# Splitting the first 4 MB load of a streaming GELU kernel by rows: 16 rows, then 112

## The chip, the cores and the metric

The kernel runs on one core of one Trainium2 chip. The metric is the device time of one execution in microseconds, as the median over several executions. Every load and store is issued by the sync engine and carried row by row by 16 DMA engines: the records of the kernel before hold 1408 packets of one row each, and 176 of 4 bytes, 16 for each of the 11 transfers. Landing times are those that the profile records.

## The reference

```python
def reference(x, y):                      # both float32, 1024 x 4096
    z = x + y
    return (0.5 * z * (1 + np.tanh(np.sqrt(2 / np.pi) * (z + 0.044715 * z ** 3)))).astype(np.float32)
```

33.55 MB are read and 16.78 MB written, with a dozen operations per element: a streaming kernel.

## The kernel before

The tensors are seen as 128 partitions of 32768 numbers. x and y come in four slabs of 128 x 8192 each (4.19 MB, 32 KB a row), alternately, all on the sync engine's queue. GpSimd adds (VectorE adds the first chunk), ScalarE and VectorE compute the GELU in chunks of 2048 columns, and three stores write the result. `begin_early` moves the first loads ahead of the program's opening barrier.

```python
    xv, yv, ov = (a.rearrange("(p n) d -> p (n d)", p=P) for a in (x, y, out))
    loads = [8192, 8192, 8192, 8192]
    stores = [16384, 10240, 6144]
    # ... (cut)
    zt = pool_sb.tile([P, TOT], fp32, tag="z", name="z")

    def load_x(i):
        a, b = lr[i]
        nc.sync.dma_start(out=zt[:, a:b], in_=xv[:, a:b])

    def load_y(i):
        a, b = lr[i]
        s, o = divmod(a, YS)
        if o == 0:
            yt[s] = pool_y.tile([P, YS], fp32, tag="y", name=f"y{s}")
        nc.sync.dma_start(out=yt[s][:, o : o + b - a], in_=yv[:, a:b])
    # ... (cut: stores, add, square, multiply-add, sigmoid, multiply; the order of issue)
    sp = []
    for i in range(len(loads)):
        sp += [(load_x, i), (load_y, i)]
    sp += [(store, i) for i in range(len(stores))]
    # ... (cut)
    tc.compile()
    begin_early(nc, 2)
    wait_late(nc)
```

Of the kernel before, what the change touches and what calls it, by code (L numbers as in the profile page):

```python
# [10 lines left out]
def begin_early(nc, count):  # L11


    head, body = (b.instructions for b in nc.main_func.blocks[:2])
    SP = mybir.EngineType.SP
    moved = [i for i in body if i.engine == SP and isinstance(i, mybir.InstDMACopy)][:count]
    assert not any(i.sync_info and i.sync_info.on_wait for i in moved)
    assert all(i.regs_accessed() == ((), ()) for i in moved)
    at = next(k for k, i in enumerate(head) if i.engine == SP)
    for k, i in enumerate(moved):  # L20
        body.remove(i)
        head.insert(at + k, i)


def wait_late(nc):



    body, end = (b.instructions for b in nc.main_func.blocks[1:3])
    last = [i for i in body if isinstance(i, mybir.InstDMACopy)][-1]  # L30
    (sem,) = [u.id for u in last.sync_info.on_update]
    all_done = end[0]
    reset = next(i for i in end if isinstance(i, mybir.InstDrain) and i.is_reset_sema)
    at = end.index(reset)
    clear = end[at + 1]
    first, stop = reset.reset_range_start, reset.reset_range_stop
    assert all_done.engine == mybir.EngineType.SP and reset.engine == mybir.EngineType.Pool
    assert isinstance(clear, mybir.InstISA) and clear.engine == mybir.EngineType.Pool
    waits = all_done.sync_info.on_wait
    (its,) = [w for w in waits if w.id == sem]  # L40

    end[0] = mybir.InstDrain(
        name=all_done.name, engine=all_done.engine, debug=all_done.debug, is_reset_sema=False,
        sync_info=mybir.SyncInfo(on_wait=[w for w in waits if w.id != sem], on_update=[]),
    )
    parts = []
    for f, e in ((first, sem), (sem + 1, stop)):
        if f < e:
            nc.gpsimd.sem_clear(range(f, e))
            parts.append(nc.cur_bb.bb.instructions.pop())  # L50
    end[at + 1 : at + 2] = parts
    end.append(
        mybir.InstEventSemaphore(
            name=clear.name, engine=mybir.EngineType.Activation, debug=clear.debug,
            sync_info=mybir.SyncInfo(
                on_wait=[its],
                on_update=[
                    mybir.SyncUpdate(
                        sync_type="semaphore", id=sem, ant_name=its.ant_name,
                        update_mode="sem-sub-imm", update_value=its.wait_value,  # L60
                    )
                ],
            ),
        )
    )
# [3 lines left out]
def kernel(  # L69
# [14 lines left out]
    nc = tc.nc  # L84
    P = nc.NUM_PARTITIONS
# [7 lines left out]
    xv, yv, ov = (a.rearrange("(p n) d -> p (n d)", p=P) for a in (x, y, out))  # L93
# [29 lines left out]
    zt = pool_sb.tile([P, TOT], fp32, tag="z", name="z")  # L123
    yt, wt, muls = {}, {}, {}

    def load_x(i):
        a, b = lr[i]
        nc.sync.dma_start(out=zt[:, a:b], in_=xv[:, a:b])  # L128

    def load_y(i):  # L130
        a, b = lr[i]
# [52 lines left out]
    for i in range(len(loads)):  # L184
        sp += [(load_x, i), (load_y, i)]
# [4 lines left out]
    for c in range(0, C, 2):  # L190
        dve += [(stt, c), (stt, c + 1), (mul, c), (mul, c + 1)]
        acts += [(sig, c), (sig, c + 1)]
        if c + 2 < C:
# [7 lines left out]
            if lr[i][0] % YS == 0  # L201
        ],
        add: lambda c: [(f, i) for i in over(lr, *cr[c]) for f in (load_x, load_y)],
        sq: lambda c: [(add, c)] + ([(mul, c - PS)] if c >= PS else []),
        stt: lambda c: [(sq, c)],
# [22 lines left out]
    ctx.close()  # L228
    tc.close()
    tc.compile()  # L230
    begin_early(nc, 2)
    wait_late(nc)


# [28 lines left out]
```

## Time and profile before

| | |
|---|---|
| time, beside the changed kernel | 120.62 us median (120.43 to 120.77, 4 runs) |
| span in the profile | 118.7 us |
| busiest compute engine | VectorE, 62% of the span |
| DMA engines occupied | 98.8% of 16 times the span |
| first load of x landed | 12.0 us |
| first load of y landed, and the first add began | 21.75 us, 21.85 us |

The table is read from below: the first add cannot start before the first slabs of x and y are there, and from the first row to the last, loads and stores occupy the 16 DMA engines almost without a gap (98.8%). The lines are shown and read in the prediction.

### The profile page before, as it was taken

To read this page: it belongs to the slowest core of one execution; us is meant where nothing else is said; L and a number is where in the kernel's file an instruction comes from. 1 tells how busy PE (TensorE), PEld (TensorE's weight loads), DVE (VectorE), ACT (ScalarE), POOL (GpSimd) and SP (SyncE) were. 2 spreads that over 40 slices of the span, in tenths; PEclk is the share of its full clock that TensorE was granted. 3 is DMA by queue.
4 is the path that set the end of the run, shared out by engine and by line. 5 is a ranking of instruction groups with operands and counts; after the bars stand their busy time and mean duration, and the time that the engine had idled before them with its cause. 6 is when DMAs were issued, how large, how long until landed. Compare 5 with 4: busy or idle time off the path is not lost.

```text
span 118.7 us, 172 instructions
## 1 busy us (share of the span) xinstructions
DVE 73.7 (62%) x35; ACT 61.0 (51%) x34; POOL 69.6 (59%) x19
## 2 busy tenths in 40 slices
DVE  0000000635799995739999968999994999990000
ACT  5000000063888965197698647888839779810000
POOL 0000000699996099999959999959999990000000
DMA  8989898989999898989999898998899889999896
GB/s 254 453 364 519 353 530 353 497 386 453 431 409 475 364 519 353 530 353 475 409 409 475 364 519 353 530 530 353 353 508 552 353 353 442 442 442 442 381 414 265
DMA packets 1584, 50.33 MB, mean 424 GB/s; under 512 B 176, under 2 KB 176, under 8 KB 176
## 3 DMA queue, kind: packets, MB, share of 16 engines
q1 hardware_dynamic: 1584, 50.33, 98.8%
HBM read 33.55 MB, written 16.78 MB: 424 GB/s over the span
## 4 chain that ended last, share of the span: by engine, by line
DMA 51%; POOL 26%; POOLq 4%; DVE 4%; DVEq 2%; ACT 2%; issue 0%; SPq 0%
DMA y<-in_y_dram 51%; POOL z L152 26%; POOLq L230 4%; DVE w L163 2%; DVEq L230 2%; DVE z L175 2%; ACT w L157 2%; SPq L128 0%; POOLq L152 0%
## 5 line engine op out<-in xcount | busy, mean ns | idle before, releaser
L152 POOL TENSOR_TENSOR z<-z,y 128x2048 f32<-128x2048 f32 x15 | 69.4, 4659 | 28.2 <-DMA y<-in_y_dram 28.2
L157 ACT ACTIVATE w<-z 128x2048 f32<-128x2048 f32 x16 | 30.1, 1882 | 37.6 <-DVE z L152 21.4
L163 DVE SCALAR_TENSOR_TENSOR w<-w,z 128x2048 f32<-128x2048 f32 x16 | 36.7, 2296 | 11.2 <-ACT w L157 11.0
L175 DVE TENSOR_TENSOR z<-w,z 128x2048 f32<-128x2048 f32 (+1 forms) x17 | 35.9, 2155 | 0.0
L168 ACT ACTIVATE w<-w 128x2048 f32<-128x2048 f32 x16 | 29.7, 1855 | 4.4 <-DVE w L163 4.3
L152 DVE TENSOR_TENSOR z<-z,y 128x2048 f32<-128x2048 f32 x1 | 2.3, 2293 | 20.5 <-DMA y<-in_y_dram 20.5
L215 ACT ACT_TABLE_LOAD x1 | 1.3, 1283 | 1.3 <-PEq L247 1.3
L214 DVE MEMSET one<- 128x1 f32 x1 | 0.1, 59 | 1.3 <-PEq L247 1.3
L247 POOL MEMSET const-float32-0.0<- 128x1 f32 x1 | 0.1, 99 | 0.2 <-issue 0.2
L215 ACT ACTIVATE one<-one 128x1 f32<-128x1 f32 x1 | 0.2, 203 | 0.0
L247 POOL MEMSET const-bfloat16-1.0<- 128x1 bf16 x1 | 0.1, 102 | 0.0
L247 POOL MEMSET const-uint8-127<- 128x1 uint8 x1 | 0.1, 102 | 0.0
L247 POOL MEMSET const-float32-1.0<- 128x1 f32 x1 | 0.1, 99 | 0.0
## 6 DMA issues: line engine op xcount, KB each, us to landing
z<-in_x_dram SPq DMA_DIRECT2D x4, 4096.0 KB, 31.3
y<-in_y_dram SPq DMA_DIRECT2D x4, 4096.0 KB, 22.2
out_dram<-z SPq DMA_DIRECT2D x1, 5120.0 KB, 15.8
out_dram<-z SPq DMA_DIRECT2D x1, 3072.0 KB, 11.9
out_dram<-z SPq DMA_DIRECT2D x1, 22.0
```

The costliest lines, as they stand in the source:

```text
L152: eng.tensor_add(out=zt[:, a:b], in0=zt[:, a:b], in1=yt[s][:, o : o + b - a])
L157: nc.scalar.activation(out=wt[c], in_=zt[:, a:b], func=act.Square, scale=root)
L163: nc.vector.scalar_tensor_tensor(out=wt[c], in0=wt[c], scalar=c1, in1=zt[:, a:b], op0=alu.add, op1=alu.mult)
L168: nc.scalar.activation(out=wt[c], in_=wt[c], func=act.Sigmoid)
L175: ins = nc.vector.tensor_mul(out=zt[:, a + o : a + o + n], in0=wt[c][:, o : o + n], in1=zt[:, a + o : a + o + n],)
L214: nc.vector.memset(one, 0.0)
L215: nc.scalar.activation(out=one, in_=one, func=act.Sigmoid)
L230: tc.compile()
L247: nc = _bacc.Bacc("TRN2", target_bir_lowering=False, num_devices=1)
```

## The change

The intent: a small transfer at the head of the queue, one row for each of the 16 DMA engines, might let the engines begin sooner than one of 128 rows. All bytes, and all work on the compute engines, stay.

```diff
     def load_x(i):
         a, b = lr[i]
-        nc.sync.dma_start(out=zt[:, a:b], in_=xv[:, a:b])
+        for r in (slice(0, 16), slice(16, P)) if i == 0 else (slice(0, P),):
+            nc.sync.dma_start(out=zt[r, a:b], in_=xv[r, a:b])
...
-    begin_early(nc, 2)
+    begin_early(nc, 3)
```

## The prediction

> **What bounds the kernel now.** I read the page first: the engine line, the slices, the DMA queue, the chain, the issues.

> ```profile
> span 118.7 us, 172 instructions
> DVE 73.7 (62%) x35; ACT 61.0 (51%) x34; POOL 69.6 (59%) x19
> ...
> DMA  8989898989999898989999898998899889999896
> ...
> q1 hardware_dynamic: 1584, 50.33, 98.8%
> ...
> DMA 51%; POOL 26%; POOLq 4%; DVE 4%; DVEq 2%; ACT 2%; issue 0%; SPq 0%
> ...
> out_dram<-z SPq DMA_DIRECT2D x1, 5120.0 KB, 15.8
> out_dram<-z SPq DMA_DIRECT2D x1, 3072.0 KB, 11.9
> out_dram<-z SPq DMA_DIRECT2D x1, 22.0
> ```

> No compute engine is above 62%, while packets occupy the 16 DMA engines for 98.8% of 16 times the span. 1.2% of 118.7 us is 1.4 us per DMA engine without a packet, start and end together. So the transfers are the bound, and nothing that leaves bytes and packet rate alone can win more than 1.4 us. The chain gives POOL 26%, which misleads: it steps through the adds because the waits allow it, not because the queue ran dry. The proof is in the times from issue to landing, from the view of tile y:

> ```profile
> L135 SPq DMA_DIRECT2D y<-in_y_dram x4: 328/376/464, 0.4 to 59.3; - x4
> ...
> DMA to landing us min/median/max: 20.7/22.2/39.5
> ```

> 50.33 MB in 0.988 x 118.7 = 117.3 us is 429 GB/s, 26.8 GB/s for each of 16 engines; a 4.19 MB load then takes 9.8 us, and one 32 KB row on one engine 1.22 us. The quickest y load needed 20.7 us from issue to landing, so it always had some 11 us of older work ahead. The three stores (8.39, 5.24 and 3.15 MB: 19.6, 12.2 and 7.3 us at that rate) landed after 22.0, 15.8 and 11.9 us: each was issued with 2.4 us or more still queued. The queue is never empty in the middle. A change of the first load therefore moves everything behind it by the same amount: what the first load loses or gains is the result.

> Then the start, as a table of stretches (duration; busy of DVE, ACT, POOL; clock; DMA share; GB/s, a packet being counted where it begins):

> ```profile
> 0.00:1.00 1.00, 0.00 (x0) 0.00 (x0) 0.20 (x4) 1.00 0.00 0
> 1.00:2.00 1.00, 0.06 (x1) 0.74 (x1) 0.00 (x0) 1.00 1.85 524
> 2.00:3.00 1.00, 0.00 (x0) 0.74 (x2) 0.00 (x0) 1.00 0.61 262
> 3.00:4.00 1.00, 0.00 (x0) 0.00 (x0) 0.00 (x0) 1.00 0.62 262
> 4.00:5.00 1.00, 0.00 (x0) 0.00 (x0) 0.00 (x0) 1.00 1.21 524
> ```

> and the timeline of the first two issues:

> ```profile
> 0.00 0.38 SPq L128 DMA_DIRECT2D z<-in_x_dram  x1
> ...
> 0.43 0.42 SPq L135 DMA_DIRECT2D y<-in_y_dram  x1
> ```

> The issue takes 0.38 us and no packet begins before 1.00. 524 GB/s in one microsecond is 0.524 MB, 16 rows of 32 KB: one first row per engine, all begun between 1.0 and 2.0. Their share of 1.85 says a first row took 1.85 us on average, 0.6 more than the steady 1.22[...]. In the packet records behind this table the first rows begin between 1.01 and 1.51 us, so the last engine starts 0.5 us after the first. This spread is what the change aims at.

> [...]

> **The change part by part.** Same bytes, same instructions on DVE, ACT and POOL; a comparison of the instruction orders shows one more transfer on the sync queue, ahead of everything, and nothing else moved.

> 1. Added: one issue, 0.38 to 0.45 us of the sync engine at the start. The y load is issued at about 0.9 instead of 0.43 us; it is not needed by the engines before about 11. Hidden.
> 2. Added: one completion write per engine. Loads land 9.7 us apart, 8 rows of 1.21 plus hardly anything; I estimate 0.03 us.
> 3. Gain:[...] The last engine sets the end, so at most 0.5 us; I estimate 0.25.
> 4. Cost, if the ports bind:[...]

> Sum: with ports binding 120.5 + 4.8 to 8.4 - 0.25 = 125.1 to 128.7, with 123.9 at the lowest (3.6 alone); without, 120.5 + 0.03 - 0.25 = 120.3.

> **The rivals.**
> - Hidden or a small gain (120.3). For it: the per-engine rate I see (26.8) is as well explained by the DMA engine as by the port[...].
> - Port contention (124 to 129).[...] Against: only that nothing here has shown it.
> - A gap between the small and the large transfer:[...] The second issue follows the first by 0.43 us, and a first row takes 1.85 us on the engine[...]; unlikely.
> - Compute becomes the bound: a slab's four adds take 17.95 us on POOL against 19.4 us for its x and y. Delayed loads delay both alike, so no. Nor do the delayed loads meet a later buffer wait: those waits end 11 us early.

> **Range and chances.** I give port contention 60%, the hidden case 38%, and a gain of over 2% (2.4 us) 2%: item 3 cannot give that, as only 1.4 us are free. The time has two humps, 120.3 and 124 to 129. I put the value at the lower part of the upper hump, **125.0 us**, and the range has to reach from one to the other: **120.1 to 129.0**.

> **What would show it.** In the changed profile, stretches between 1 and 8 us decide. With contention[...] the small transfer lands near 7 us instead of about 4, the large one at 16 to 20 instead of 12, the first add begins at 26 to 30 instead of 21.85, and every later landing is late by the same amount, with the DMA share still near 99%. Without it the second rows begin by 3.2 us, the first add within 0.3 us of 21.85. Step 3 is right if the first rows begin within 0.1 us of each other. I am wrong if the delay appears but is made up later (then the queue was not as full as I say), or if landings are on time and the end is not.

The sum came to 125.1 to 128.7 us with contention and 120.3 us without. The cut item gave it the terms 4.8 and 8.4 us (3.6 us for the "at the lowest" case): 120.5 + 4.8 - 0.25 = 125.1 and 120.5 + 8.4 - 0.25 = 128.7. "Port" is the word for whatever rows that slow each other have in common; no run shows what that is.

## The result, and the profile after

The changed kernel took **130.19 us** in the median (130.04 to 130.73, 4 runs), the kernel before 120.62 us. The ratio is 1.080 (95% interval 1.077 to 1.084). Ratios here are the mean time of one kernel's fast runs over that of the other's fast runs of the same rounds, so they are not quite the ratio of the medians. Executions over 1.5% slower than the fastest of the same kernel are left out of the means. The result is correct.

From the page of the changed kernel: span, compute engines, DMA slices, packets of the DMA queue, and the small transfer's issue.

```profile
span 129.1 us, 173 instructions
## 1 busy us (share of the span) xinstructions
DVE 73.7 (57%) x35; ACT 61.0 (47%) x34; POOL 69.6 (54%) x19
...
GB/s 162 162 162 315 264 223 315 447 376 477 437 386 477 437 386 477 416 396 487 396 416 487 396 416 477 396 426 508 386 548 366 386 548 307 470 457 406 376 434 190
...
q1 hardware_dynamic: 1600, 50.33, 98.4%
...
z<-in_x_dram SPq DMA_DIRECT2D x1, 512.0 KB, 7.6
```

Compute is busy for the same 73.7, 61.0 and 69.6 us as before. The DMA engines are still "occupied" for 98.4%, of a span that is 10.4 us longer with the same bytes. So they don't idle: they hold their packets longer. The slices say when: the first seven (3.2 us each) move 162 to 315 GB/s, the later ones about what the kernel before moves, whose slices (3.0 us each) are

```profile
GB/s 254 453 364 519 353 530 353 497 386 453 431 409 475 364 519 353 530 353 475 409 409 475 364 519 353 530 530 353 353 508 552 353 353 442 442 442 442 381 414 265
```

The DMA share alone would have hidden this; share and GB/s have to be read together.

The same stretches of the start as a table (duration; busy time of DVE, ACT and POOL; clock; DMA share; GB/s, with a packet counted where it begins), first before:

```profile
3.00:6.00 3.00, 0.00 (x0) 0.00 (x0) 0.00 (x0) 1.00 1.01 437
6.00:12.00 6.00, 0.00 (x0) 0.00 (x0) 0.00 (x0) 1.00 1.01 437
12.00:20.00 8.00, 0.00 (x0) 0.00 (x0) 0.00 (x0) 1.00 1.00 430
```

and after:

```profile
1.00:2.00 1.00, 0.06 (x1) 0.27 (x1) 0.00 (x0) 1.00 3.76 524
2.00:3.00 1.00, 0.00 (x0) 1.00 (x1) 0.00 (x0) 1.00 0.00 0
3.00:6.00 3.00, 0.00 (x0) 0.22 (x2) 0.00 (x0) 1.00 1.04 175
6.00:12.00 6.00, 0.00 (x0) 0.00 (x0) 0.00 (x0) 1.00 0.75 191
12.00:20.00 8.00, 0.00 (x0) 0.00 (x0) 0.00 (x0) 1.00 1.02 254
```

In both kernels 16 rows begin between 1 and 2 us. Before, each takes 1.85 us on average; after, 3.76, and no engine begins another row before 3.0 us. Then the 112 rows run at 175 to 254 GB/s where the kernel before has 430. The first add tells what that costs, before

```profile
21.85 2.29 DVE L152 TENSOR_TENSOR z<-z,y 128x2048 f32<-128x2048 f32 x1 [20.46 <-DMA y<-in_y_dram]
```

and after:

```profile
32.34 2.29 DVE L153 TENSOR_TENSOR z<-z,y 128x2048 f32<-128x2048 f32 x1 [30.48 <-DMA y<-in_y_dram]
```

It is 10.5 us late. In the records of landings the first x slab comes at 22.50 instead of 12.04 us, the first y slab at 32.21 instead of 21.75, the last y slab at 90.48 instead of 80.02, the last store at 129.05 instead of 118.66: 10.5, 10.5, 10.5 and 10.4 us. The loss arises in the first load and nothing is made up or added later.

### The profile page after: what moved, and what is told of

Read it like the earlier page. It is cut to its first block, busy times and chain, and to the rows that moved or that the text cites. A ratio compares the mean times of both kernels' runs of the same rounds, so it can differ in the third digit from the quotient of the medians.

```text
span 129.1 us, 173 instructions
## 1 busy us (share of the span) xinstructions
DVE 73.7 (57%) x35; ACT 61.0 (47%) x34; POOL 69.6 (54%) x19
## 2 busy tenths in 40 slices
DMA packets 1600, 50.33 MB, mean 390 GB/s; under 512 B 192, under 2 KB 192, under 8 KB 192
## 3 DMA queue, kind: packets, MB, share of 16 engines
q1 hardware_dynamic: 1600, 50.33, 98.4%
## 4 chain that ended last, share of the span: by engine, by line
DMA 42%; POOL 33%; issue 4%; POOLq 4%; DVE 3%; DVEq 2%; ACT 1%; SPq 1%
DMA y<-in_y_dram 42%; POOL z L153 33%; POOLq L231 4%; DVE w L164 2%; DVEq L231 2%; DVE z L176 2%; ACT w L158 1%; SPq L129 1%; POOLq L153 0%
## 5 line engine op out<-in xcount | busy, mean ns | idle before, releaser
L164 DVE SCALAR_TENSOR_TENSOR w<-w,z 128x2048 f32<-128x2048 f32 x16 | 36.7, 2296 | 11.1 <-ACT w L158 10.9
## 6 DMA issues: line engine op xcount, KB each, us to landing
out_dram<-z SPq DMA_DIRECT2D x1, 5120.0 KB, 15.7
out_dram<-z SPq DMA_DIRECT2D x1, 3072.0 KB, 11.9
```

The lines of the kernel that those rows point to most:

```text
L164: nc.vector.scalar_tensor_tensor(out=wt[c], in0=wt[c], scalar=c1, in1=zt[:, a:b], op0=alu.add, op1=alu.mult)
```

## The experiments

### The same split by columns

A small transfer first, too, but with all 128 partitions in both parts.

```diff
-        for r in (slice(0, 16), slice(16, P)) if i == 0 else (slice(0, P),):
-            nc.sync.dma_start(out=zt[r, a:b], in_=xv[r, a:b])
+        for o, e in ((a, a + 1024), (a + 1024, b)) if i == 0 else ((a, b),):
+            nc.sync.dma_start(out=zt[:, o:e], in_=xv[:, o:e])
```

> The first load of x is split as well, and again a small transfer comes first (0.5 MB), but by columns: 128 rows of 4 KB, then 128 rows of 28 KB. All 128 partitions in both. Port theory (the loss comes from which partitions are written together): no loss, 120.6 us, between 120.3 and 120.9. Rival, that a further transfer or a small one at the head of the queue costs the 10 us: about 130 us.

Measured: 120.83 us against 120.41 (ratio 1.002, interval 1.001 to 1.004). Neither the further transfer nor the small one at the head costs 10 us. Nor does either help.

### The row split, but of the second load of x

```diff
-        for r in (slice(0, 16), slice(16, P)) if i == 0 else (slice(0, P),):
+        for r in (slice(0, 16), slice(16, P)) if i == 1 else (slice(0, P),):
...
-    begin_early(nc, 3)
+    begin_early(nc, 2)
```

> The same 16 and 112 rows, but of the second load of x, in the middle of a full queue. Port theory: the same loss as at the start, 129 to 131 us. Rival, that the loss belongs to the start[...]: 120.5 us, within 0.5.

Measured: 130.63 us against 120.41 (1.084). The loss is the same in the middle of a full queue, so it does not come from the start.

### The two parts in the other order

```diff
-        for r in (slice(0, 16), slice(16, P)) if i == 0 else (slice(0, P),):
+        for r in (slice(16, P), slice(0, 16)) if i == 0 else (slice(0, P),):
```

> The two transfers of the change in the other order: 112 rows, then 16. Port theory: the same rows meet at the same ports, 129 to 131.5 us. Rival, that the cost comes from the small transfer holding up the head of the queue: it now stands behind 112 rows, at most 1 us of loss, 120.5 to 121.5.

Measured: 130.52 us against 120.36 (1.085). The order does not matter; the small transfer is not a plug at the head of the queue.

### Two times 64 rows: lower and upper half, then even and odd rows

Everything countable is equal (two transfers, 64 rows each, 2 MB each, 4 rows per DMA engine); only which rows travel together differs.

```diff
-        for r in (slice(0, 16), slice(16, P)) if i == 0 else (slice(0, P),):
+        for r in (slice(0, 64), slice(64, P)) if i == 0 else (slice(0, P),):      # halves
+        for r in (slice(0, P, 2), slice(1, P, 2)) if i == 0 else (slice(0, P),):  # even and odd
```

> The first load of x as rows 0 to 63 and rows 64 to 127. Port theory:[...] 19.4 instead of 9.7 us: 130.2 us (129 to 131.5). Rival, that the loss comes from a very small transfer (16 rows) or from a row count that is no power of two (112): 64 rows are neither, 4 to an engine, 120.6 us.

> The first load of x as two transfers of 64 rows again, but even rows and odd rows in place of the lower and the upper half. Sizes, row counts, rows per engine and number of transfers are those of the 64/64 split, which took 131.0 us; only the rows that travel together differ[...]. The probe of every second row landed 7.6 us after its issue, against 12.6 for 64 neighbouring rows. Port theory: 120.5 us, within 0.4. Rival, that row-split transfers are slow as such: about 131 us.

Measured: halves 131.01 us against 120.41 (1.088); even and odd rows 120.84 us against 120.36 (1.004, interval 1.003 to 1.005). By the count of groups above the lower half has 8 of them, and so has the upper, while the even rows have all 16; probes of the three sets took 12.6, 12.7 and 7.6 us. The table of stretches for the halves:

```profile
4.00:8.00 4.00, 0.00 (x0) 0.00 (x0) 0.00 (x0) 1.00 0.92 188
8.00:12.00 4.00, 0.00 (x0) 0.00 (x0) 0.00 (x0) 1.00 1.16 246
```

and for even and odd rows:

```profile
5.00:8.00 3.00, 0.00 (x0) 0.00 (x0) 0.00 (x0) 1.00 0.81 350
8.00:12.00 4.00, 0.00 (x0) 0.00 (x0) 0.00 (x0) 1.00 1.18 508
```

Some 215 GB/s, on average over 4 to 12 us, against 440 over 5 to 12 us. This shows the cause: which rows travel together. That it is the side written, the partitions, and not the rows of x that are read, the probes below show. A small loss remains, 0.4% for even and odd rows and 0.2% for the column split. With even and odd rows the first y slab lands 0.3 us later than before (22.08 against 21.75), and the packet records show where that arises: the first rows begin at 1.34 to 2.30 us in place of 1.01 to 1.51, after a first issue of 0.55 us in place of 0.38. Why that issue is longer is not shown.

### What each shape of load costs

Seventeen and sixteen loads of 32 KB rows were put ahead of the kernel before, into the place that its last x slab fills later; each waits for the one before to land.

```diff
+        nc.sync.dma_start(out=zt[0:4, TOT - YS :], in_=xv[0:4, TOT - YS :])
+        nc.sync.dma_start(out=zt[0:128:32, TOT - YS :], in_=xv[0:4, TOT - YS :])
+        nc.sync.dma_start(out=zt[0:16:4, TOT - YS :], in_=xv[0:4, TOT - YS :])
+        ... (further shapes)
...
-    begin_early(nc, 2)
+    begin_early(nc, 0)
```

> The kernel before with 17 loads of x ahead of it, each of 32 KB rows into the place that the fourth load fills later, each issued only when the one before has landed; the result stays right and the total time means nothing. From issue to landing, port theory = 1.21 us times the larger of rows per engine and rows per port, plus 2.3 us: 4 rows into partitions 0-3[...] 7.1 us, into 0,32,64,96[...] 4.7, into 0,4,8,12[...] 3.5; 16 rows into 0-15 7.1; the same 16 partitions fed from every eighth row of x 7.1; 16 rows into every eighth partition[...] 4.7; 32 rows 7.1; 64 rows 12.0; 112 rows at least 12.0 and up to 15 with clashes; 96 rows at least 12.0; 128 rows 12.0. Rival, DMA engines alone (rows per engine): 4 rows 3.5 in all three places, 16 rows 3.5, 32 rows 4.7, 64 rows 7.1, 96 rows 9.6, 112 rows 10.8. Rival, the side of the memory that is read (which rows of x are fetched together): 16 rows slow when fetched from rows 0-15 into any partitions, and quick from every eighth row.

> Sixteen more loads ahead of the kernel before, each issued when the one before has landed, to learn how rows are dealt to the engines. From issue to landing, 2.2 us plus 1.21 times the larger of rows per engine and rows per port, if no rows clash by timing: every fourth row[...] 4.6; rows 0,2,..62[...] 7.1;[...] rows 0,4,..28[...] 3.4; rows 0-7[...] 7.1; 48 rows at least 9.5; 80 rows at least 12; every second of 0-95 (48 rows) 7.1; every second of 0-111 (56 rows) 7.1; 120 rows[...] 12 or more; rows 16-111 16.6 as rows 0-95. What lies above these is clashes that depend on the dealing. Neighbouring rows dealt one after the other to each engine would make 128 rows 21 us, which they are not (11.9).

The sync engine's timeline of the first of these kernels (start, duration, line) shows the issues; an issue waits for the landing of the one above it, so the distance between two starts is what the upper one took:

```profile
12.70 0.34 SPq L217 DMA_DIRECT2D z<-in_x_dram  x1
18.76 0.63 SPq L218 DMA_DIRECT2D z<-in_x_dram  x1
23.36 0.60 SPq L219 DMA_DIRECT2D z<-in_x_dram  x1
27.18 0.33 SPq L220 DMA_DIRECT2D z<-in_x_dram  x1
33.97 0.56 SPq L221 DMA_DIRECT2D z<-in_x_dram  x1
...
97.92 0.32 SPq L228 DMA_DIRECT2D z<-in_x_dram  x1
115.62 0.32 SPq L229 DMA_DIRECT2D z<-in_x_dram  x1
```

Line 217 is the load of the same 4 rows of x into partitions 0 to 3, line 218 into 0, 32, 64, 96, line 219 into 0, 4, 8, 12: 6.1, 4.6 and 3.8 us for the same bytes from the same addresses. Line 220 is 16 rows into partitions 0 to 15 (6.8 us), line 228 the 112 rows of the change (17.7 us). In the table, the right column takes off the 2.2 us by which 128 rows (11.9 us) exceed 8 rows of 1.21 us.

| rows written | groups by the count above | issue to landing, us | without 2.2 us |
|---|---|---|---|
| 4: partitions 0-3 / 0, 32, 64, 96 / 0, 4, 8, 12 | 1 / 2 / 4 | 6.1 / 4.6 / 3.8 | 3.9 / 2.4 / 1.6 |
| 8: partitions 0-7 / every fourth of 0-28 | 2 / 8 | 6.2 / 3.7 | 4.0 / 1.5 |
| 16: partitions 0-15 / every eighth | 4 / 8 | 6.8 / 5.0 | 4.6 / 2.8 |
| 16: partitions 0-15, from every eighth row of x | 4 | 6.8 | 4.6 |
| 16: every fourth of 0-60 / every second of 0-30 | 8 / 8 | 4.8 / 5.0 | 2.6 / 2.8 |
| 32: 0-31 / every second of 0-62 / every fourth | 8 / 8 / 16 | 7.2 / 7.4 / 5.0 | 5.0 / 5.2 / 2.8 |
| 64: 0-63 / 64-127 / even partitions, from rows 0-63 of x | 8 / 8 / 16 | 12.6 / 12.7 / 7.6 | 10.4 / 10.5 / 5.4 |
| 48: 0-47 | 8 | 14.2 | 12.0 |
| 48: every second of 0-94 | 16 | 9.2 | 7.0 |
| 56: every second of 0-110 | 16 | 12.5 | 10.3 |
| 80: 0-79 | 12 | 14.0 | 11.8 |
| 96: 0-95 / 16-111 | 16 / 16 | 16.6 / 16.4 | 14.4 / 14.2 |
| 112: 16-127, from rows 16-127 or 0-111 of x | 16 | 17.7 / 17.7 | 15.5 / 15.5 |
| 112: 0-111 | 16 | 15.9 | 13.7 |
| 120: 0-119 | 16 | 22.3 | 20.1 |
| 128 | 16 | 11.9 to 12.1 | 9.7 to 9.9 |

Three things follow. For 4 to 32 rows and for 64, the port theory's figures hold to about 1 us, the largest miss being partitions 0 to 3 (6.1 us, not 7.1). Which rows of x are read makes no difference (16 and 112 rows; and the same rows 0 to 63 of x take 12.6 us into partitions 0 to 63, but 7.6 into the even ones), so the reading side is out. But the other counts cost more: every second of 0-94 (48 rows) and of 0-110 (56 rows) were both expected at 7.1 us and took 9.2 and 12.5, and 112 rows, expected at 12 to 15, took 17.7. That is far more than their rows per group: without the 2.2 us, 112 rows were to cost 9.7 us at the least (8 rows of 1.21 us in the fullest group), and 10.9 us by the stepping (an estimate from the same 1.21 us, with every engine at the pace of its own group), and cost 15.5. Counting groups does not explain this, as 56, 96 and 112 rows reach all 16.

### Do engines at free groups run on?

My stepping assumed that they do. A transfer of 16 rows has one row per engine (16 begin together, 524 GB/s in 1 us), so its clashes can be counted without knowing how rows are dealt. By the count above, every seventh partition from 0 to 105 gives 12 rows with a group of their own and two pairs that share one (0 with 35, 28 with 63). Three such loads were queued without waits, into three slabs.

```diff
+        nc.sync.dma_start(out=zt[0:112:7, 1 * YS : 2 * YS], in_=xv[0:112:7, 1 * YS : 2 * YS])
+        nc.sync.dma_start(out=zt[0:112:7, 2 * YS : 3 * YS], in_=xv[0:112:7, 2 * YS : 3 * YS])
+        nc.sync.dma_start(out=zt[0:112:7, 3 * YS : 4 * YS], in_=xv[0:112:7, 3 * YS : 4 * YS])
+        ... (whole loads, then the same with every third partition of 0 to 45, and whole loads again)
```

> Ahead of the kernel before: three loads in a row of the same 16 rows, every seventh partition from 0 to 105, one row per engine in each[...]. Then, between loads of all rows, three of every third partition from 0 to 45[...]. Each-for-itself theory: in the first three, 12 engines need 1.21 us a row and 4 need 2.4. Together theory: all 16 need 2.4 us a row. Every third: 1.2, 2.4 and 3.6 us side by side, or 3.6 for all.

The table of stretches over these three loads:

```profile
14.00:15.00 1.00, 0.00 (x0) 0.00 (x0) 0.00 (x0) 1.00 2.16 524
15.00:15.80 0.80, 0.00 (x0) 0.00 (x0) 0.00 (x0) 1.00 0.00 0
15.80:17.30 1.50, 0.00 (x0) 0.00 (x0) 0.00 (x0) 1.00 1.66 350
17.30:18.20 0.90, 0.00 (x0) 0.00 (x0) 0.00 (x0) 1.00 0.00 0
18.20:19.70 1.50, 0.00 (x0) 0.00 (x0) 0.00 (x0) 1.00 1.66 350
```

524 GB/s in 1 us and 350 in 1.5 are 0.524 MB each, exactly 16 rows: all 16 engines begin the second row in one stretch and the third in another, and none begins a row between. 12 engines at free groups would have begun their third row 1.21 us after the second. In the packet records each of the 16 takes 2.45 to 2.48 us for the second row. In the other kind of load (every third partition, 1 to 3 rows to a group) each takes 4.26 us for the second row, where 3.6 had been expected. **In these loads all engines go together, at the pace of the most crowded group.** The each-for-itself theory has fallen. The pace is not 1.21 us times the rows in that group, though: a row takes 1.21 us with one to a group, 2.47 with two, 4.26 with three and 4.50 with four (the last from the run of eight times 16 rows below). These loads read every seventh or third row of x as well, which was not varied by itself.

An estimate by this rule: if neighbouring rows are dealt in turn to each of 16 engines (3, 5, 6, 7 rows), the most crowded group has 3 engines at every step for 48 rows and 2 for 80, 96 and 112. At 1.2 us per row in a group that makes 10.8, 12.0, 14.4 and 16.8 us, against 12.0, 11.8, 14.4 and 15.5 measured. It also gives 7.2 us for the 48 strided rows, against 7.0. It fails for some other loads (see "Open"). The rule was then put to the test on a split that had not been run:

```diff
-        for r in (slice(0, 16), slice(16, P)) if i == 0 else (slice(0, P),):
+        for r in (slice(0, 48), slice(48, P)) if i == 0 else (slice(0, P),):
```

> The first load of x as rows 0-47 and rows 48-127. Two ways to count the clashes, both with neighbouring rows dealt one after the other to an engine (3 and 5 each). Together theory: all 16 engines advance at the pace of the most crowded port of the moment[...]: 23.8 us by the probes for the first load instead of 9.7, so 134.5 us (133 to 135.5). Each-for-itself theory, as in the prediction (an engine at a free port runs on at full pace): 9.6 + 10.8 = 20.4 us, so 131.2 us. If only the number of rows per port counted[...]: 130 us at most.

Measured: 134.41 us against 120.42 (1.115). It separates the theories by 3 us and agrees with the together theory, and with the sum of the two probes. As a test of times it is not quite a fresh one: the forecast of 134.5 us is that sum of probes, and the rule's own 22.8 us would give 133.5. The packet records of this run say more. After the first 16 rows of each part, a row of the 48 takes 4.01 to 4.14 us and a row of the 80 takes 2.36 to 2.46, whichever row it is.

### Eight times 16 rows

```diff
-        for r in (slice(0, 16), slice(16, P)) if i == 0 else (slice(0, P),):
+        for r in [slice(r, r + 16) for r in range(0, P, 16)] if i == 0 else (slice(0, P),):
...
-    begin_early(nc, 3)
+    begin_early(nc, 8)
```

> The first load of x as 8 transfers of 16 neighbouring rows[...]. One such transfer was measured at 6.8 us from issue to landing, 4.6 without the latency. Port theory: 8 x 4.6 = 37 us for the first load in place of 9.7, so 147 us (142 to 150). Rival, a cost per extra transfer that I read off the change (10 us for one more): 7 more would make 190; rival, that the 112-row transfer alone is ill (15.4 of the 20 us): without one, 120.5 + 3.6 at most.

Measured: 146.79 us against 120.36 (1.219, from 2 runs). Each of the eight transfers lies in four groups by the count above; the loss is 26.4 us where 8 x 4.6 - 9.7 = 27.1 was expected. Neither a fixed cost per transfer (190 us) nor an ill of the 112-row shape alone (124 us) fits.

No run beats the kernel before. Nor do the runs point to one that would: the small transfer does not start sooner (next section), and a split that spreads over the groups gains nothing (columns 0.2% and even and odd rows 0.4% slower).

## Why the prediction was right or wrong

**What bounds the kernel, and that the queue is full: right.** The landings moved by the same 10.4 to 10.5 us down to the last store, and the DMA share stayed at 98.4%. One of the proofs was weaker than it was read: the first load of the probes, with nothing ahead of it, landed 2.2 us later than its eight rows take, so a store that needs 2.4 us beyond its transfer shows hardly any older work.

**Step 1 (the extra issue is hidden): right.** The y load is issued at 0.90 us, as foretold.

**Step 2 (0.03 us per further transfer): too high, but without weight.** The completions show in the records as 4-byte packets at the end of a transfer, 16 for each (176 before, 192 after), and one takes 0.01 us on average. The two harmless splits lost 0.4 to 0.5 us, so nearly all of that is something else.

**Step 3 (a smaller transfer narrows the engines' start): wrong.** In the packet records the first rows begin between 1.03 and 1.72 us, against 1.01 and 1.51 before. So 16 rows start neither sooner nor closer together, and the change has no gain to lose.

**Step 4, port contention: that these rows slow each other was right, and one term was mis-sized.** The figures that follow are estimates from 1.2 us a row. The 16 rows were put at 4.8 us; the probe says 4.6. The term that failed is the time of the 112 rows. The slowest engine was to finish both parts at 18.1 us, by a stepping row by row that let every engine at a free group run on. Its 18.1 us is also a slip: worked through again by the same rule, it gives 4.8 us for the 16 rows and 10.9 for the 112, 15.7 us together and a loss of 6.0, not 8.4. The 112 rows took 15.5 us, not 10.9 (nor the 13.3 that the 18.1 leaves for them). What the runs show in its place is that engines at free groups don't run on: where the rows per group could be counted, all 16 went at the pace of the most crowded one (2.47 us a row with two to a group). That the same makes up the whole of the 15.5 us is argued, as the dealing of the 112 rows is not recorded and the rule gives 16.8. With the measured terms the sum is 4.6 + 15.5 - 9.7 = 10.4 us, which is the delay seen in the landings. The top of my range, 129.0 us, rested on the 8.4 us; without the slip the same sum ends at 126.3, further still from the 130.2 measured.

**The rivals.** "Hidden or a small gain" had 38% and was wrong: the 16 rows of the small transfer are in flight together and take 3.76 us each, against 1.85 before. The gap between the two transfers and compute as the bound were rightly put aside: the engines are occupied throughout.

**Open.** How the rows of a transfer are dealt to the engines is not shown by the records, which don't name the engine. Neighbouring rows in turn fit 48, 80 and 96 rows to 1.2 us, but the same rule would make 128 rows 19 us, 64 even rows 9.7 and every fourth row 4.8, which measure 9.7, 5.4 and 2.8, so it does not hold for these. For 56 and 120 rows (10.3 and 20.1 us) no estimate is given, as it is not shown how many engines carry them. For 112 rows the rule is too high: it gives 16.8 us for partitions 16 to 127 and 0 to 111 alike, which took 15.5 and 13.7. In their packet records (the first probe kernel) the rows take between 1.2 and 2.7 us, so there the engines don't go in step at two rows to a group all the time. Why three rows to a group cost nearly as much as four (4.26 and 4.50 us a row) is open too. And why an engine at a free group waits for the others is not shown, only that it does.

## What to carry to other kernels

In a kernel like this one, which the DMA engines bound, split a load by columns (0.2% lost) rather than into groups of neighbouring partitions: 128 rows took 9.7 us where 112 took 15.5. If rows must be split, let each part be spread over all partitions (even and odd rows lost 0.4%, halves 8.8%). And read the DMA share together with GB/s: the share stayed at 98% while the rate in the first load fell to half or less.
